# A GLA and Conformer trunk on one core: even tokens first, side taps on one chain, and an earlier rank for a block's last scaling

## The chip, the cores and the metric

The kernel runs on one core of one Trainium2 chip. The metric is the device time of one execution in microseconds (us). A core has five instruction queues that matter here, each working in order: TensorE (PE, matmuls), VectorE (DVE), ScalarE (ACT), GpSimd (POOL) and SyncE (SP), which issues every DMA of this kernel.

## The reference

Two residual layers over 2048 tokens of width 1024, and a last RMSNorm, all in float32:

```python
for i in range(DEPTH):                     # DEPTH = 2
    h = rmsnorm(x, norm_w[i])
    y = gla_mixer(h, ...) if i % 2 == 0 else conv_mixer(h, ...)
    x = x + y
return rmsnorm(x, final_norm_w)

def conv_mixer(h, ...):
    a, gl, z = jnp.split(h @ w_in, 3, axis=-1)
    u = a * jax.nn.sigmoid(gl)
    u = causal_depthwise_conv(u, dw_w) + dw_b          # 31 taps
    u = jax.nn.silu(layernorm(u, ln_w, ln_b))
    return (u * jax.nn.silu(z)) @ w_out
```

The first layer is gated linear attention with four heads in chunks of 64 tokens. The second is the causal convolution module above.

## The kernel before

Activations lie with channels on the partitions and tokens along the free axis. The sequence is done in two halves of 1024 tokens (`hf`), each half in two blocks of 512 (`b`). Every projection is made of three matmuls per pair of 128x128 weights, since both operands are split in a high and a low part (`mm3`, L144): 24 matmuls of 512 columns fill one bank of the pool `ps_mm`, which has three banks. Weights come in units of 256 columns: SP loads `wr` (L123), ACT copies it to `wh` (L124), POOL makes the rest `wl` (L125), one unit ahead of its use.

Up to about 900 us the first layer runs. Its head outputs `g` are transposed on PE (L413), copied by ACT and stored to `g_scratch`, and read back by `out1`, which adds the input again from `xT` and stores `x1_scratch`.

Then the second layer runs, `in2(0)`, `in2(1)`, `out2(0)`, `out2(1)`. In `in2` each channel tile `c` of eight gets a gated `u` (L754, VectorE reads a bank of `ps_mm` and so frees it). The convolution is done for pairs of tokens: `u` holds even tokens in `ue` and odd ones in `uo`, three chains A (16 taps, on `ue`), B (15 taps, on `uo`) and C (16 taps, on `ue+uo` with summed weights) give the even output A+B and the odd output C-A-B. A tap is one multiply-add on VectorE (L638) with its running sum in a bank of the pool `ps_b` (two banks). The first `nside` taps of A and of B are made elsewhere: ACT multiplies (L622, L620) and POOL adds (L624), in SBUF tiles `convA` and `convB`; the chain on VectorE takes that sum up at its first tap (L642). C starts from A's sum in SBUF (L640). POOL adds A+B (L647, `even`); `ue+uo` (L669) is POOL's in the first half and VectorE's in the second. The table `SIDES` gives `nside` by half and tile.

The layer norm over the eight tiles (`centre` L700 to L709, `norm` L727 to L729) runs in the background of later projections. In the second half its norms come while `out2(0)` multiplies; their results `yb` are the operands of `out2(1)`.

`out2(hf)` does two blocks of four units; each project loads `x1` into a tile (L825), adds the bank to it (L838), and sums squares (L842, L844). After the fourth unit `finish` makes the factor of the last RMSNorm on PE and POOL, scales the eight tiles in place (L864) and stores them. Block 0 of either half takes its `x1` tiles from the three `u` buffers and the two `prod` buffers, so block 0 of the second half loads into tiles that block 0 of the first half must first have scaled and stored.

The order of each engine's instructions is made when the kernel is built: the framework plans a timeline from its own durations and takes, among what it holds ready, what ranks highest; `tc.high_priority(offset=n)` puts the instructions inside n places ahead of their place in the program. `pump` hands out the background items by a credit of TensorE time.

Of the kernel before, what the change touches and what calls it, by code (L numbers as in the profile page):

```python
# [13 lines left out]
P = 128  # L14
D = 1024
# [15 lines left out]
SIDES = ((1, 7, 7, 7, 7, 5, 9, 7),  # L31
         (1, 5, 3, 5, 9, 7, 6, 4))
# [8 lines left out]
def kernel(  # L41
    ctx: ExitStack,
    tc: tile.TileContext,
    xT: bass.AP,
    wall: bass.AP,
# [21 lines left out]
    ps_m = ctx.enter_context(tc.tile_pool(name="ps_m", bufs=3, space=bass.MemoryType.PSUM))  # L67

# [296 lines left out]
    def core(hf, h, i, v, sz, qkb, sink):  # L365
# [40 lines left out]
        def turn():  # L406
            g = sink.pop(("g", i))
            if i % 2 == 0:
                sink["t"] = m_bank()
            gt = sink["t"]  # L410
            for c in range(2):
                o = c * 256 + (i % 2) * P
                pe.transpose(gt[:, o:o + P], g[:, c * P:(c + 1) * P], ident)  # L413
            if i % 2 == 1:
                st = t2("st")
                for c in range(2):
                    cs = slice(c * 256, (c + 1) * 256)
                    act.activation(st[:, cs], gt[:, cs], AF.Copy, scale=cc(C_GN, 2 * h + c))
                if h < HEADS - 1:
                    for c in range(2):  # L420
                        r0 = (2 * h + c) * P
                        sp.dma_start(
                            out=gd[hf, r0:r0 + P, (i - 1) * P:(i + 1) * P],
                            in_=st[:, c * 256:(c + 1) * 256])
                else:
                    sink["stage"].append(st)
# [67 lines left out]
    def out1(hf, stage, ahead):  # L494
        a = [[], []]
        for b in range(2):
            if b == 1:
                run_late(0)
            for k in range(KT):
# [6 lines left out]
                else:  # L506
                    for s in range(2):
                        src = stage[b * 2 + s][:, (k - 6) * 256:(k - 5) * 256]
                        ds = slice(s * 256, (s + 1) * 256)
                        act.activation(hi[:, ds], src, AF.Copy)  # L510
                        dve.tensor_tensor(lo[:, ds], src, hi[:, ds].bitcast(F32), ALU.subtract)
                a[b].append((hi, lo))
        accs = [l1p.tile([P, NB], F32, name="acc", bufs=2) for _ in range(2)]
        for pair in range(2):
            ws = [next_unit(12 + 2 * pair), next_unit(13 + 2 * pair)]
            for b in range(2):
                t0 = hf * TH + b * NB
                for ch in range(4 * pair, 4 * pair + 4):
                    xr = l1p.tile([P, 4, 3, CK], F32, name="Q", bufs=2).rearrange("p a b c -> p (a b c)")[:, 0:NB]
                    sp.dma_start(out=xr, in_=xT[ch * P:(ch + 1) * P, t0:t0 + NB])  # L520
# [77 lines left out]
    def conv(hf, c, u, dst, S1):  # L598
# [13 lines left out]
        def side(which):  # L612

            st[which] = l2p.tile([P, NB + 1], F32, name="conv" + which, bufs=2)
            acc = st["p" + which] = st[which][:, 1:NB + 1]
            for m in range(nside):
                src, w = tap(which, m)
                p = acc if m == 0 else l2p.tile([P, NB], F32, name="prod", bufs=2)
                if m == 0 and which == "B":
                    act.activation(p, src, AF.Identity, scale=w, bias=cc(C_DWB, c))  # L620
                else:
                    act.activation(p, src, AF.Copy, scale=w)  # L622
# [3 lines left out]
        def chain(which, m0, m1, n):  # L626
            def fn():
                first = 0 if which == "C" else nside
                if m0 == first:
                    st["ps"] = b_bank()  # L630
                ps = st["ps"]
# [19 lines left out]
        def odd():  # L651
            dve.scalar_tensor_tensor(
                dst[c][:, 1], st["ps"], dwb2[:, c:c + 1], st["B"][:, 1:NB + 1], ALU.add, ALU.subtract)
# [8 lines left out]
        for which, n in (("A", 16), ("B", 15), ("C", 16)):  # L662
            m0 = 0 if which == "C" else nside
# [4 lines left out]
            if which == "A":  # L668
                items.append((0.0, lambda: (pool if hf == 0 else dve).tensor_tensor(ue, ue, uo, ALU.add)))  # L669
            if which == "B":  # L670
                items.append((0.0, even))
        items.append((0.7, odd))
        items.append((0.0, sums))
        side("A")
        side("B")
# [3 lines left out]
    def layernorm(hf, dst, S1, y_out):  # L679
# [41 lines left out]
        def norm(b, k):  # L721
            def fn():
                z = b2()
                sp.dma_start(out=z, in_=szd[hf, k * P:(k + 1) * P, b * NB:(b + 1) * NB])
                zv = z.rearrange("p (t s) -> p s t", s=2)
# [16 lines left out]
    def in2(hf, sched, a, y_out, ahead):  # L742
        dst, S1 = [], []

        def glu(w, u, b):
            with tc.high_priority(offset=PRIO):
# [8 lines left out]
                    u[:, :, o:o + 256].rearrange("p s t -> p t s"),  # L755
                    a_ps.rearrange("p (t s) -> p t s", s=2),
                    sg.rearrange("p (t s) -> p t s", s=2), ALU.mult)
# [46 lines left out]
    def out2(hf, a):  # L804
        for b in range(2):
# [41 lines left out]
            def finish(s):  # L847
                ss = slice(s * n, (s + 1) * n)
                kp = () if ns == 1 else (1, 3, 5) if s else (1, 3, 5, 7)
                with tc.high_priority(offset=1000 if ns > 1 else 0):  # L850
# [6 lines left out]
                for ch, m, t in parts:  # L857
                    for k in range(ch, ch + m):
                        x = xs[k][:, ss]
                        if k in kp:  # L860
                            act.activation(x, x, AF.Copy, scale=cc(C_FW, k))
                            pool.tensor_tensor(x, x, rbs, ALU.mult)
                        else:
                            dve.scalar_tensor_tensor(x, x, cc(C_FW, k), rb, ALU.mult, ALU.mult)  # L864
                    sp.dma_start(
                        out=out[ch * P:(ch + m) * P, t0 + s * n:t0 + (s + 1) * n].rearrange("(c p) t -> p c t", p=P),
                        in_=t[:, :, ss])
# [120 lines left out]
```

## Time and profile before

| | us |
|---|---|
| median of 3 runs | 1676.16 |
| lowest and highest of them | 1675.92, 1680.72 |
| the profiled execution, its own time | 1678.1 |
| its span, first to last instruction | 1676.0 |

All views of the trace come from the profiled execution and count from the start of its span. Names are the program's with buffer numbers left out, L12 is line 12 of the kernel before. "Idle before" names the engine that ended a wait. The granted TensorE clock is given as a share: 1.00 is 2.4 GHz, 0.50 is 1.2 GHz.

### The profile page before, as it was taken

What the parts mean: (1) busy time and instruction counts of PE and PEld (TensorE: products, weight loads), DVE (VectorE), ACT (ScalarE), POOL (GpSimd) and SP (SyncE); (2) the same over time, 40 slices, a digit from 0 to 9 for tenths busy, and PEclk for the clock granted to TensorE, in tenths of its full rate; (3) what the DMA queues carried; (4) which work ended last, traced back from release to release, by engine and by line L of the source; (5) the groups of instructions that cost most, each with busy time, mean ns of one, the idle gap of its engine ahead of it and who ended that gap; (6) DMA issues with size and microseconds to landing.
All of it is one profiled execution on the core that took longest, in us unless ns stands there. A gap on an engine that the chain in (4) does not pass through costs nothing.

```text
span 1676.0 us, 23547 instructions
## 1 busy us (share of the span) xinstructions
PE 1609.4 (96%) x9028; PEld 1410.2 (84%) x9028; DVE 972.7 (58%) x1481; ACT 739.6 (44%) x1246; POOL 900.2 (54%) x787
## 2 busy tenths in 40 slices
PE   8999999999999999999999999999999899999697
PEld 6989999998889999999888887877788678877597
DVE  7433232241434232325243999989699999977634
ACT  6645252342557353415232544443553355435432
POOL 4444343334744333323342989985398798456342
PEclk9999999999999999999999999999999999999798
DMA  6021111144511212123452211225154113643633
GB/s 190 26 83 57 64 51 57 57 139 139 169 45 33 82 51 64 45 63 102 144 164 88 76 38 38 94 70 157 59 174 157 57 45 101 202 163 124 234 115 137
DMA packets 74016, 165.68 MB, mean 99 GB/s; under 512 B 7760, under 2 KB 16464, under 8 KB 73904
## 3 DMA queue, kind: packets, MB, share of 16 engines
q1 hardware_dynamic: 73904, 164.19, 30.5%
q8 instruction: 70, 1.15, 0.3%
q14 instruction: 42, 0.34, 0.1%
HBM read 128.51 MB, written 35.65 MB: 98 GB/s over the span
## 4 chain that ended last, share of the span: by engine, by line
PE 73%; DVE 16%; DMA 3%; ACT 3%; issue 2%; POOL 2%; SPq 0%; POOLq 0%; DVEq 0%; ACTq 0%
PE mm L144 63%; DVE pb L638 10%; PE pb L144 3%; PE pb L388 1%; PE pb L390 1%; DVE pb L642 1%; PE pm L379 1%; DMA wr<-in_wall_dram 1%; PE pm L413 1%; DVE u L754 1%; DVE al L190 1%; PE pm L288 1%; POOL acc L205 1%; DMA u<-x_scratch 1%; DVE pb L640 1%
## 5 line engine op out<-in xcount | busy, mean ns | idle before, releaser
L144 PE MATMUL mm<-ah,wh 128*128 128x512 f32 (+1 forms) x1600 | 595.3, 388 | 44.8 <-DVE u L838 20.4
L144 PE MATMUL mm<-al,wh 128*128 128x512 f32 (+1 forms) x1600 | 592.6, 385 | 0.0
L144 PE MATMUL mm<-ah,wl 128*128 128x512 f32 (+1 forms) x1600 | 590.0, 386 | 0.0
L125 POOL TENSOR_TENSOR wl<-wr,wh 128x1024 fp32r<-128x1024 f32 x140 | 344.0, 2471 | 214.9 <-ACT wh L124 208.9
L144 PEld LDWEIGHTS mm<-ah,wh 128*128 128x128 f32 x1600 | 302.3, 190 | 110.1 <-DVE u L838 20.0
L144 PEld LDWEIGHTS mm<-al,wh 128*128 128x128 f32 x1600 | 302.2, 190 | 57.1 <-issue 0.2
L144 PEld LDWEIGHTS mm<-ah,wl 128*128 128x128 f32 x1600 | 301.4, 190 | 58.0 <-issue 0.2
L144 PE MATMUL mm<-wh,ah 128*128 128x256 f32 x896 | 259.2, 289 | 0.0
L144 PE MATMUL mm<-wh,al 128*128 128x256 f32 x896 | 254.7, 284 | 0.0
L144 PE MATMUL mm<-wl,ah 128*128 128x256 f32 x896 | 254.2, 284 | 0.0
L124 ACT ACTIVATE wh<-wr 128x1024 fp32r<-128x1024 f32 x144 | 145.5, 1051 | 140.9 <-PE mm L144 92.4
L638 DVE SCALAR_TENSOR_TENSOR pb<-u,C,pb 128x512 f32<-128x512 f32 x252 | 184.9, 747 | 0.7
L638 DVE SCALAR_TENSOR_TENSOR pb<-u,dwc,pb 128x512 f32<-128x512 f32 x240 | 179.9, 750 | 1.2
L144 PEld LDWEIGHTS mm<-wl,ah 128*128 128x128 f32 x896 | 171.4, 191 | 0.4
L144 PEld LDWEIGHTS mm<-wh,ah 128*128 128x128 f32 x896 | 171.3, 191 | 0.4
L144 PEld LDWEIGHTS mm<-wh,al 128*128 128x128 f32 x896 | 171.3, 191 | 0.0
L622 ACT ACTIVATE prod<-u,C 128x512 f32<-128x512 f32 x148 | 105.5, 721 | 135.7 <-POOL convA L624 68.4
L624 POOL TENSOR_TENSOR convA<-convA,prod 128x512 f32<-128x512 f32 x74 | 98.3, 1329 | 5.7 <-ACT prod L622 1.6
L624 POOL TENSOR_TENSOR convB<-convB,prod 128x512 f32<-128x512 f32 x74 | 98.0, 1325 | 4.0 <-ACT convB L620 0.7
L397 DVE SCALAR_TENSOR_TENSOR S<-S,dec,pb 128x256 f32<-128x256 f32 x56 | 26.8, 479 | 95.4 <-PE pb L144 95.3
L401 POOL TENSOR_TENSOR ss<-ss,e 128x1 f32<-128x1 f32 x64 | 13.4, 209 | 124.4 <-ACT g L400 124.4
L523 DVE TENSOR_TENSOR Q<-mm,Q 128x512 f32<-128x512 f32 x32 | 22.1, 689 | 93.0 <-PE mm L144 78.3
(195 smaller groups left out, 2174.1 us busy)
## 6 DMA issues: line engine op xcount, KB each, us to landing
wr<-in_wall_dram SPq DMA_DIRECT2D x144, 512.0 KB, 4.1
raw<-in_xT_dram SPq DMA_DIRECT2D x32, 256.0 KB, 3.7
Q<-in_xT_dram SPq DMA_DIRECT2D x32, 256.0 KB, 3.2
x_scratch<-Q SPq DMA_DIRECT2D x32, 256.0 KB, 3.1
sz_scratch<-t SPq DMA_DIRECT2D x32, 256.0 KB, 2.3
b<-sz_scratch SPq DMA_DIRECT2D x32, 256.0 KB, 3.5
g_scratch<-st SPq DMA_DIRECT2D x48, 128.0 KB, 1.9
raw<-g_scratch SPq DMA_DIRECT2D x24, 256.0 KB, 3.5
```

What stands on the lines that cost most here:

```text
L124: act.activation(wh[:, ks, :], raw, AF.Copy)
L125: (dve if i < 2 else pool).tensor_tensor(wl[:, ks, :], raw, wh[:, ks, :].bitcast(F32), ALU.subtract)
L144: pe.matmul(ps, s, m, start=(i == 0), stop=(i == 3 * n - 1))
L190: dve.tensor_tensor(lo, src, hi.bitcast(F32), ALU.subtract)
L205: eng.tensor_tensor(acc, acc, sq, ALU.add)
L288: pe.matmul(ps, wgs[:, k, :], m, start=(n == 0), stop=(n == 15))
L379: pe.matmul(s_ps[:, 0:192], ki[:, js], Q[:, j].rearrange("p s c -> p (s c)"), start=True, stop=True)
L397: dve.scalar_tensor_tensor(S[h], S[h], dec[:, j:j + 1], kv, ALU.mult, ALU.add)
L523: dve.tensor_tensor(xr, ps, xr, ALU.add)
L622: act.activation(p, src, AF.Copy, scale=w)
L624: pool.tensor_tensor(acc, acc, p, ALU.add)
L638: dve.scalar_tensor_tensor(dstm, src, w, ps, ALU.mult, ALU.add)
```

## The change

Three things change. First, tokens are kept even ones first inside each block of 512, from the head outputs on: the transposes of `g` write their columns apart, the stores to `g_scratch` go in rows of 128 elements instead of 256, `out1` reads its residual from a copy `xP` of the input in that order, and the host puts the output back in order. With that `u`, the gate and `z` are read and written in two runs of 256 in place of steps of two. Second, POOL and ACT make side taps for A alone (the table holds about the double of the old one), B starts on VectorE with its bias, A keeps its sum in the bank, VectorE makes the even output from that bank, and C goes on in the same bank; `ue+uo` is POOL's in both halves. Third, the factor of `finish` ranks 1000 ahead in every block, and its scaling and stores rank `PRIO` (80) ahead.

```diff
-SIDES = ((1, 7, 7, 7, 7, 5, 9, 7),
-         (1, 5, 3, 5, 9, 7, 6, 4))
+SIDES = ((2, 14, 14, 14, 14, 10, 15, 14),
+         (2, 10, 6, 10, 15, 14, 12, 8))
...
-                o = c * 256 + (i % 2) * P
-                pe.transpose(gt[:, o:o + P], g[:, c * P:(c + 1) * P], ident)
+                o = (i % 2) * CK
+                gv = gt[:, c * 256:(c + 1) * 256].rearrange("p (s t) -> p s t", s=2)[:, :, o:o + CK]
+                pe.transpose(gv.rearrange("p s t -> p t s"), g[:, c * P:(c + 1) * P], ident)
...
-        def side(which):
+        def side():
...
+            acc = st["pA"] = l2p.tile([P, NB], F32, name="convA", bufs=2)
             for m in range(nside):
-                src, w = tap(which, m)
+                src, w = tap("A", m)
...
                 for m in range(m0, m1):
                     src, w = tap(which, m)
-                    dstm = ps
-                    if m == n - 1 and which != "C":
-                        dstm = st["p" + which]
+                    dstm = st["B"][:, 1:NB + 1] if which == "B" and m == n - 1 else ps
                     if m > first:
                         dve.scalar_tensor_tensor(dstm, src, w, ps, ALU.mult, ALU.add)
-                    elif which == "C":
-                        dve.scalar_tensor_tensor(dstm, src, w, st["pA"], ALU.mult, ALU.subtract)
+                    elif which == "A":
+                        dve.scalar_tensor_tensor(dstm, src, w, st["pA"], ALU.mult, ALU.add)
+                    elif which == "B":
+                        dve.tensor_scalar(dstm, src, w, cc(C_DWB, c), ALU.mult, ALU.add)
                     else:
-                        dve.scalar_tensor_tensor(dstm, src, w, st["p" + which], ALU.mult, ALU.add)
+                        dve.scalar_tensor_tensor(dstm, src, w, ps, ALU.mult, ALU.subtract)
...
-            pool.tensor_tensor(d[:, 0], st["pA"], st["B"][:, 0:NB], ALU.add)
+            dve.tensor_tensor(d[:, 0], st["psA"], st["B"][:, 0:NB], ALU.add)
...
-        for which, n in (("A", 16), ("B", 15), ("C", 16)):
+        for which, n in (("B", 15), ("A", 16), ("C", 16)):
...
-                items.append((0.0, lambda: (pool if hf == 0 else dve).tensor_tensor(ue, ue, uo, ALU.add)))
+                items.append((0.0, lambda: pool.tensor_tensor(ue, ue, uo, ALU.add)))
+                items.append((0.6, even))
...
-                with tc.high_priority(offset=1000 if ns > 1 else 0):
+                with tc.high_priority(offset=1000):
...
-                for ch, m, t in parts:
-                    for k in range(ch, ch + m):
+                with tc.high_priority(offset=PRIO):
+                    for ch, m, t in parts:
+                        for k in range(ch, ch + m):
```

Where the instructions stand now is shown at three places. The first is VectorE in the second half, where one tile's chain ends and the next one's goes on (`d<-pb,dwb` is the odd output, `u<-u` is `ue+uo`, taps with `dwc` are C's). Before:

```order
L638 SCALAR_TENSOR_TENSOR convA<-u,C,pb 128x512
L652 SCALAR_TENSOR_TENSOR d<-pb,dwb_96,convB 128x512
L669 TENSOR_TENSOR u<-u 128x527
L642 SCALAR_TENSOR_TENSOR pb<-u,C,convB 128x512
L640 SCALAR_TENSOR_TENSOR pb<-u,dwc,convA 128x512
L638 SCALAR_TENSOR_TENSOR pb<-u,C,pb 128x512
L638 SCALAR_TENSOR_TENSOR pb<-u,dwc,pb 128x512
```

and now (L637 is a tap, L639 A's first, L641 B's first, L643 C's first, L648 the even output):

```order
L637 SCALAR_TENSOR_TENSOR convB<-u,C,pb 128x512
L637 SCALAR_TENSOR_TENSOR pb<-u,dwc,pb 128x512
L639 SCALAR_TENSOR_TENSOR pb<-u,C,convA 128x512
L653 SCALAR_TENSOR_TENSOR d<-pb,dwb_96,convB 128x512
L648 TENSOR_TENSOR d<-pb,convB 128x512
L641 TENSOR_SCALAR pb<-u,C 128x512
L637 SCALAR_TENSOR_TENSOR pb<-u,C,pb 128x512
L643 SCALAR_TENSOR_TENSOR pb<-u,dwc,pb 128x512
```

Of a tile's three first taps, one has its sum in SBUF (`convA`) now and not three; B starts from `u` and constants alone; the even output has come to VectorE and `ue+uo` has left it.

The second is VectorE in `out2(0)`, with the norms of the second half (`d<-d,pm` are eight scalings of one block by the layer norm's factor, `b<-b,d` products with the gate, `v4n` that factor's first step, `v` that of `finish`, `u<-u,C,pb` and `prod<-prod,C,pb` the last scaling). Before, from the norm factor of block 1 on:

```order
L167 TENSOR_SCALAR v4n<-pm 128x4
L838 TENSOR_TENSOR d<-mm,d 128x512 x3
L167 TENSOR_SCALAR v_14037<-pb 128x4
L727 TENSOR_TENSOR d<-d,pm 128x2x256 x8
L729 TENSOR_TENSOR b_13753<-b_13753,d 128x2x256
L729 TENSOR_TENSOR b_13812<-b_13812,d 128x2x256
...
L844 TENSOR_TENSOR acc<-acc,pb 128x512 x2
L729 TENSOR_TENSOR b_13830<-b_13830,d 128x2x256
...
L729 TENSOR_TENSOR b_13848<-b_13848,d 128x2x256
L864 SCALAR_TENSOR_TENSOR u<-u,C,pb 128x512 x2
...
L864 SCALAR_TENSOR_TENSOR u<-u,C,pb 128x512 x4
L864 SCALAR_TENSOR_TENSOR prod<-prod,C,pb 128x512 x2
```

and now, from the norms of block 0 on to the same factor `v4n`:

```order
L729 TENSOR_TENSOR b_13666<-b_13666,d 128x512
L709 TENSOR_TENSOR S_12023<-S_12023,pb 128x2x256
...
L729 TENSOR_TENSOR b_13721<-b_13721,d 128x512
L844 TENSOR_TENSOR acc<-acc,pb 128x512
L192 TENSOR_TENSOR al<-b_13708,ah 128x512
L865 SCALAR_TENSOR_TENSOR u<-u,C,pb 128x512 x5
...
L865 SCALAR_TENSOR_TENSOR prod<-prod,C,pb 128x512 x2
L844 TENSOR_TENSOR acc<-acc,pb 128x512
L192 TENSOR_TENSOR al<-b_13734,ah 128x512
L838 TENSOR_TENSOR d<-mm,d 128x512
L169 TENSOR_SCALAR v4n<-pm 128x4
```

The eight scalings of block 0 stood behind the norms of block 1, and stand now ahead of that block's factor.

The third is SP's queue at the same place (`wr` are weights, `b<-sz_scratch` gates for the norms, `d` and `u` the loads of `x1`). Before:

```order
L123 DMA wr<-in_wall_dram 128x1024 x3
L825 DMA d<-x_scratch 128x2x512 x4
L123 DMA wr<-in_wall_dram 128x1024
...
L123 DMA wr<-in_wall_dram 128x1024
L865 DMA out_dram<-u 128x2x512
L123 DMA wr<-in_wall_dram 128x1024
L865 DMA out_dram<-u 128x2x512
L825 DMA u<-x_scratch 128x2x512
L865 DMA out_dram<-u 128x2x512
L865 DMA out_dram<-prod 128x512 x2
L825 DMA u<-x_scratch 128x2x512 x2
```

and now:

```order
L724 DMA b_13807<-sz_scratch 128x512
L866 DMA out_dram<-u 128x2x512 x2
L825 DMA u<-x_scratch 128x2x512
L724 DMA b_13816<-sz_scratch 128x512
L866 DMA out_dram<-u 128x2x512
L866 DMA out_dram<-prod 128x512
L825 DMA u<-x_scratch 128x2x512
L866 DMA out_dram<-prod 128x512
L125 DMA wr<-in_wall_dram 128x1024
L724 DMA b_13825<-sz_scratch 128x512
L125 DMA wr<-in_wall_dram 128x1024
L825 DMA u<-x_scratch 128x2x512
```

The stores of block 0's result and the loads into its tiles stand now ahead of two loads of weights and of the loads of `d`.

## Rows read from the trace of the kernel before

**Rows 1.** The page, busy time: us (share of span)
```profile
PE 1609.4 (96%) x9028; PEld 1410.2 (84%) x9028; DVE 972.7 (58%) x1481; ACT 739.6 (44%) x1246; POOL 900.2 (54%) x787
```

**Rows 2.** Stretches: length, busy us by engine, granted TensorE clock, DMA
```profile
0.00:900.00 900.00, 886.88 (x5679) 809.93 (x5680) 328.81 (x583) 398.08 (x755) 371.20 (x420) 1.00 0.29 89
900.00:1000.00 100.00, 100.00 (x453) 83.13 (x451) 76.41 (x105) 41.95 (x59) 70.10 (x55) 1.00 0.13 43
1000.00:1200.00 200.00, 188.68 (x803) 153.24 (x802) 183.69 (x241) 90.73 (x131) 150.51 (x111) 0.97 0.27 85
...
1300.00:1490.00 190.00, 178.46 (x766) 144.95 (x765) 183.66 (x249) 82.44 (x112) 137.20 (x93) 0.98 0.35 111
1490.00:1560.00 70.00, 66.51 (x298) 54.44 (x297) 52.05 (x76) 41.39 (x63) 45.74 (x25) 0.95 0.41 134
1560.00:1590.00 30.00, 13.81 (x56) 11.24 (x55) 18.93 (x28) 9.07 (x15) 8.10 (x4) 0.72 0.79 275
```

**Rows 3.** Waits of TensorE, 900 to 1500: who for whom, us, times, longest
```profile
PE mm L144 <- DVE u L754: 12.6, 6, 4.4
PE mm L144 <- DVE u L838: 4.2, 4, 1.8
PE mm L144 <- ACT t L767: 3.1, 1, 3.1
```

**Rows 4.** Groups by form, 930 to 1676: busy us, mean ns, idle before
```profile
L638 DVE SCALAR_TENSOR_TENSOR pb<-u,C,pb 128x512 f32<-128x512 f32 x248 | 182.3, 747 | 0.7
...
L624 POOL TENSOR_TENSOR convA<-convA,prod 128x512 f32<-128x512 f32 x74 | 98.3, 1329 | 5.7 <-ACT prod L622 1.6 <-ACT convA L622 0.7
...
L640 DVE SCALAR_TENSOR_TENSOR pb<-u,dwc,convA 128x512 f32<-128x512 f32 x16 | 26.0, 1626 | 0.0
...
L754 DVE TENSOR_TENSOR u<-mm,t 128x512 f32<-128x512 f32 x29 | 30.1, 1071 | 2.7 <-PE mm L144 2.7
...
L642 DVE SCALAR_TENSOR_TENSOR pb<-u,C,convB 128x512 f32<-128x512 f32 x15 | 25.7, 1715 | 5.2 <-POOL convB L624 5.2
...
L647 POOL TENSOR_TENSOR d<-convA,convB 128x512 f32<-128x512 f32 x16 | 22.3, 1397 | 27.0 <-DVE convB L638 25.9 <-ACT prod L622 1.2
L642 DVE SCALAR_TENSOR_TENSOR pb<-u,C,convA 128x512 f32<-128x512 f32 x15 | 20.3, 1356 | 0.0
...
L669 DVE TENSOR_TENSOR u<-u 128x527 f32<-128x527 f32 x8 | 11.2, 1399 | 0.0
L669 POOL TENSOR_TENSOR u<-u 128x527 f32<-128x527 f32 x8 | 11.1, 1391 | 0.3 <-DVE convA L638 0.3
...
L838 DVE TENSOR_TENSOR u<-mm,u 128x512 f32<-128x512 f32 x12 | 8.0, 685 | 20.6 <-PE mm L144 14.2 <-DMA u<-x_scratch 6.5
```

**Rows 5.** Waits of VectorE, 1040 to 1200
```profile
DVE pb L642 <- POOL convB L624: 5.2, 1, 5.2
```

**Rows 6.** Chain that ended last, 1540 to 1600: start us, us, what
```profile
1570.08 1.41 DVE u L864 x2
...
1571.50 3.56 DMA out_dram<-u
...
1575.08 6.19 DMA u<-x_scratch
...
1581.36 0.70 DVE u L838
```

**Rows 7.** TensorE alone, 1564 to 1588
```profile
1564.00:1588.00 24.00, 7.81 (x29) 0.64 0.81 280
```

**Rows 8.** Timeline of VectorE, 1480 to 1600: start us, us, what
```profile
1521.21 4.87 DVE L727 TENSOR_TENSOR d<-d,pm 128x512 f32<-128x512 f32 x8 [0.94 <-PE pm L178]
...
1548.70 4.87 DVE L727 TENSOR_TENSOR d<-d,pm 128x512 f32<-128x512 f32 x8 [0.66 <-PE pm L178]
```

**Rows 9.** The stretch 1000 to 1100, all engines
```profile
1000.00:1100.00 100.00, 97.38 (x428) 79.79 (x427) 99.08 (x134) 49.14 (x70) 97.02 (x74) 1.00 0.22 74
```

**Rows 10.** Groups by line, 0 to 930: the transposes of g
```profile
L413 PE MATMUL pm<-ident,g 128*128 128x128 f32 x128 | 24.4, 272 | 0.0
```

More of the change, by code (lines that the diff above doesn't have):

```diff
@@ L44 @@
     xT: bass.AP,
+    xP: bass.AP,
     wall: bass.AP,
@@ L421, in turn @@
                         r0 = (2 * h + c) * P
+                        b, o = i // 4, (i % 4 // 2) * P
                         sp.dma_start(
-                            out=gd[hf, r0:r0 + P, (i - 1) * P:(i + 1) * P],
-                            in_=st[:, c * 256:(c + 1) * 256])
+                            out=gd[hf, r0:r0 + P, b * NB:(b + 1) * NB].rearrange(
+                                "p (s t) -> p s t", s=2)[:, :, o:o + P],
+                            in_=st[:, c * 256:(c + 1) * 256].rearrange("p (s t) -> p s t", s=2))
                 else:
@@ L507, in out1 @@
                     for s in range(2):
[L508 to L511, printed above, removed]
+                        src = stage[b * 2 + s][:, (k - 6) * 256:(k - 5) * 256].rearrange("p (s t) -> p s t", s=2)
+                        h2, l2 = (t.rearrange("p (s t) -> p s t", s=2)[:, :, s * P:(s + 1) * P] for t in (hi, lo))
+                        act.activation(h2, src, AF.Copy)
+                        dve.tensor_tensor(l2, src, h2.bitcast(F32), ALU.subtract)
                 a[b].append((hi, lo))
@@ L519, in out1 @@
                     xr = l1p.tile([P, 4, 3, CK], F32, name="Q", bufs=2).rearrange("p a b c -> p (a b c)")[:, 0:NB]
-                    sp.dma_start(out=xr, in_=xT[ch * P:(ch + 1) * P, t0:t0 + NB])
+                    sp.dma_start(out=xr, in_=xP[ch * P:(ch + 1) * P, t0:t0 + NB])
                     ps = mm_bank()
@@ L610, in tap @@
             return ue[:, m:m + NB], dwc[:, c, m:m + 1]
-        def side(which):
-            st[which] = l2p.tile([P, NB + 1], F32, name="conv" + which, bufs=2)
-            acc = st["p" + which] = st[which][:, 1:NB + 1]
+        def side():
+            acc = st["pA"] = l2p.tile([P, NB], F32, name="convA", bufs=2)
             for m in range(nside):
-                src, w = tap(which, m)
+                src, w = tap("A", m)
                 p = acc if m == 0 else l2p.tile([P, NB], F32, name="prod", bufs=2)
[L619 to L622, printed above, removed]
+                act.activation(p, src, AF.Copy, scale=w)
                 if m > 0:
@@ L652, in odd @@
             dve.scalar_tensor_tensor(
-                dst[c][:, 1], st["ps"], dwb2[:, c:c + 1], st["B"][:, 1:NB + 1], ALU.add, ALU.subtract)
+                dst[c][:, 1], st["psA"], dwb2[:, c:c + 1], st["B"][:, 1:NB + 1], ALU.add, ALU.subtract)
         def sums():
@@ L661, in conv @@
         items = []
-        for which, n in (("A", 16), ("B", 15), ("C", 16)):
-            m0 = 0 if which == "C" else nside
+        for which, n in (("B", 15), ("A", 16), ("C", 16)):
+            m0 = nside if which == "A" else 0
             while m0 < n:
@@ L668, in conv @@
             if which == "A":
-                items.append((0.0, lambda: (pool if hf == 0 else dve).tensor_tensor(ue, ue, uo, ALU.add)))
-            if which == "B":
-                items.append((0.0, even))
+                items.append((0.0, lambda: pool.tensor_tensor(ue, ue, uo, ALU.add)))
+                items.append((0.6, even))
         items.append((0.7, odd))
         items.append((0.0, sums))
-        side("A")
-        side("B")
+        side()
+        st["B"] = l2p.tile([P, NB + 1], F32, name="convB", bufs=2)
         pool.tensor_copy(st["B"][:, 0:1], bcar[:, c:c + 1])
```

39 lines of the change are left out of this document (21 added, 18 removed).

## The prediction

> **What bounds the kernel now.** I read the page first: TensorE is busy 96% of the span [rows 1], so little more than the rest can be won, and the question is where that rest lies. The table of stretches says it [rows 2]. Before 900 us TensorE is idle for 13.1 us of 900. From 1000 to 1200 it lacks 11.3 us and from 1300 to 1490 another 11.5; in both VectorE is busy 183.7 us, 92% and 97% of the stretch. From 1560 to 1590 it lacks 16.2 us, over half of that stretch. These are two different limits, and the change touches both.
>
> The first is the convolution. Of these 22.9 us of TensorE's waits 12.6 and 4.2 end with VectorE [rows 3], which reads a bank of `ps_mm` late because taps stand ahead of that read in its queue; the rest, 6.1, are ACT's, half of it one wait of 3.1. The granted clock falls behind such waits: 0.97 of 200 us and 0.98 of 190 us [rows 2] is another 9.8 us of work at 2.4 GHz not done. So the convolution's stage loses about 32.7 us, and VectorE's share by the waits is 16.8/22.9 of it, 24 us.
>
> The second is one wait. The chain shows it [rows 6]: the last scaling of block 0 on VectorE starts at 1570.1, its first two take 1.41 us, the store from that tile 3.56, the load of new `x1` into it 6.19, the add that frees the bank 0.70; TensorE goes on at 1582.1. From 1564 to 1588 it made 29 matmuls [rows 7], where a stretch without waits makes 453 in 100 us, 0.22 us each [rows 2]; 80 are missing, 17.6 us, of which 16.2 are the wait and the rest the half clock behind it.
>
> **The change, part by part.** VectorE first, per channel tile [rows 4]. The three first taps cost 1.356 (A), 1.715 (B) and 1.626 us (C), each with two operands in SBUF; an ordinary tap, whose sum is in a bank, costs 0.747. Now only A's first tap reads a sum in SBUF. C's starts from the bank: 0.747. B's starts from `u` and two constants, a form that the trace doesn't show; between the add's 0.685 and 1.356 I take 0.747, since its one operand is less than a tap has. That is 4.70 before and 2.85 now, 1.85 less. The even output comes to VectorE; its form is that of the residual add, a bank and an SBUF tile to SBUF, 0.685. The two writes of `u` cost 1.071 each with steps of two; in two runs they are the same add, 0.685 each, 0.77 less, or nothing less if the steps are not what costs. Together 1.93 us less per tile, 31 us for 16 tiles. In the second half eight sums `ue+uo` leave VectorE, 8 x 1.399 = 11.2. The table gives 174 side taps for 180, so VectorE gets six more taps, 4.5 us. In all VectorE loses 37.6 us of work, 13 in the first half and 24 in the second; 25 in all at the worst end of the writes.
>
> That VectorE and POOL take the same for `ue+uo`, 1.399 and 1.391 us, is a row of this trace [rows 4]. The Trainium skill says otherwise (GPSIMD Engine Reference, section Key points): VectorE is about twice as fast at elementwise work. By that rule the eight sums would be an estimated 5.6 us on VectorE and the work taken from it 32 us; the trace differs, with 1.399, and I go by it.
>
> POOL, on the other side: 158 side adds for 148 at 1.329, 16 even outputs at 1.397 less, eight more sums at 1.391 [rows 4]: 4.5 us less in the first half, 6.6 more in the second. In the first half it has no room, busy 97.0 of 100 us from 1000 to 1100 [rows 9]; in the second it has (137.2 of 190, [rows 2]), which covers its 6.6 us. ACT makes six activations fewer and bounds nothing.
>
> What of this reaches the end? In the first half 13 us are freed against a loss of 17.3 (11.3 idle, 6 of clock), in the second 24 against 15.3, and only the part that VectorE ends counts: 12 and 11, 23 us if all goes. I take three quarters, **17 us**: some of TensorE's waits come from single long stays in VectorE's queue that a smaller sum doesn't remove, and A's first tap now needs POOL's whole side sum, where the old chain began after half of it. The stall that VectorE itself had there, 5.2 us for B's side sum [rows 5], goes, as B has none; A's first tap is late next. Bounds: 8 us, if only that stall and the clock behind it go, and 24.
>
> Then the last scaling. By the order rows, the scaling of block 0 stands now ahead of the norm factor of block 1; it stood behind the eight scalings that began at 1548.7 [rows 8]. Counted from the norm of block 0, which ends at 1526.1 [rows 8], sixteen instructions stand before it, at 0.6 (an eighth of 4.87, [rows 8]) to 1.1 us (a write of `u`, [rows 4]) each, 10 to 18 us: it starts at 1536 to 1544. The chain behind it (1.41 + 3.56 + 6.19 + 0.70, 11.9 us) then ends by 1556, before 1565.9 (1582.1 less 16.2), where TensorE ran out of banks. So the wait and its clock go, 17.6 us. I give back 3 us: eight scalings (5.6 us at 0.70) stand ahead of block 0's last splits, and in SP's queue the stores and two loads, which wait for the scaling and for a store of 3.56 us, stand ahead of two loads of weights. Leaves **14.5 us**, between 11 and 17.6. The norms of block 1 come later by some 6 us; they are needed eight projections after TensorE enters `out2(1)`, 8 x 24 x 0.22 = 42 us, and that is their cover. If it is gone, each further us is a wait.
>
> The rest I cost at nothing. The transposes have as many columns as before. The stores of `g` have rows half as long, but they are of heads 0 to 2 and are read only after head 3. `xP` is read as `xT` was. The norms' product with the gate gets plainer steps, below 1 us in all on the path.
>
> The sum: 17 + 14.5 = 31.5 us. Against the profiled execution's span of 1676.0 us that is 1644.5; its own time was 1678.1, but the median of the runs, 1676.16, is what I count from: **1645 us**.
>
> **The rivals.** *POOL takes VectorE's place.* For it: 97.0 of 100 us in the first half [rows 9], and one chain of up to fifteen side taps that must be whole before A starts. Against it: POOL's own sum falls by 4.5 us there, and fifteen taps of B stand before A on VectorE as cover. Then about 3 us of the 17 are left: 1676.2 - 14.5 - 3 = 1659. *The wait at the scaling comes back elsewhere*: the norms of block 1, or the weights behind the stores, are late for `out2(1)`. For it: VectorE, SP and POOL each work in order and all carry both; against: the 42 us of cover. Then only some 2 us of the second part are left: 1676.2 - 17 - 2 = 1657. *The new order doesn't bring what it says*: the builder's plan puts the items in order by its own durations, and where the chip's differ, waits move and don't go. Both parts nearly lost: 1674, no change. *Slower:* the transposes. They now write every column apart by 512 bytes from the one before, a form that no row shows on TensorE. There are 128, at 0.272 us [rows 10], in a stretch where TensorE is busy 886.9 of 900 us [rows 2], so nothing covers them. It decides from 31.5/128 = 0.25 us more for each, nearly a doubling: at twice 0.272 the time is 1676.2 - 31.5 + 34.8 = 1679.5, at three times 1714. Against it: the count of columns and weights is the same, and nothing in the trace ties a matmul's time to where it writes.
>
> **How the numbers follow.** Forecast 0.55, POOL 0.17, wait elsewhere 0.13, no change 0.08, slower 0.07. The forecast's own range is 1635 to 1657 (24 + 17.6 and 8 + 11 us). With the two rivals that keep one part it reaches 1664, and 3 us are added below for a write of `u` or a first tap of B that is cheaper than its bound: 1632 to 1664 holds 0.85. A measurement of this kernel can tell about 0.3%, 5 us, from no change; faster by more than that are the first three cases, 0.85, within it 0.08, slower 0.07.
>
> **What would show it.** In the changed kernel's profile VectorE's busy time is about 935 us (972.7 less 37.6); the writes of `u` take about 0.69 us, C's first tap 0.75, only A's first tap over 1.3. TensorE's waits for the write of `u` fall from 12.6 us to under 5. The wait of 16.2 us is gone, and the scaling of block 0 stands some 10 us behind the norms of that block. Wrong: VectorE waits for `convA` by over 5 us (POOL); TensorE waits as long for the weights or for the splits of `out2(1)` (wait elsewhere); transposes over 0.35 us.

## The result, and the profile after

The changed kernel takes 1653.85 us, the median of 4 runs (1652.13 to 1657.52), against 1676.04 of the kernel before: ratio 0.9866, 95% interval 0.9839 to 0.9892. It is 22.2 us faster, for 31.5 predicted; the time lies in the range. The profiled execution's span is 1650.7 us, for 1676.0, 25.3 less; one execution lies some us off the median.

The page of the changed kernel, its first part (engine, busy us and share of the span, instructions), which answers to [rows 1]:

```profile
PE 1603.1 (97%) x9028; PEld 1406.7 (85%) x9028; DVE 954.5 (58%) x1495; ACT 739.4 (45%) x1244; POOL 889.0 (54%) x789
```

VectorE's busy time falls by 18.2 us, half of the 37.6 that were forecast. The table of stretches (columns as in [rows 2]):

```profile
1000.00:1200.00 200.00, 191.90 (x828) 156.38 (x826) 181.77 (x256) 91.11 (x131) 144.83 (x112) 0.98 0.28 89
1300.00:1490.00 190.00, 186.25 (x805) 152.67 (x804) 176.81 (x257) 81.93 (x115) 132.39 (x90) 0.98 0.36 119
1490.00:1560.00 70.00, 64.15 (x306) 53.06 (x305) 57.44 (x78) 43.68 (x65) 48.34 (x25) 0.98 0.59 202
1560.00:1590.00 30.00, 28.80 (x144) 24.18 (x143) 21.40 (x28) 10.97 (x16) 14.86 (x8) 1.00 0.57 205
```

In both convolution stretches TensorE makes more matmuls than in [rows 2], and in 1560 to 1590 it is busy 28.8 of 30 us, where it was 13.8. The waits of TensorE from 900 us to the end:

```profile
PE mm L146 <- ACT t L767: 4.3, 3, 3.0
PE mm L146 <- DVE u L838: 4.3, 2, 3.1
PE mm L146 <- ACT t L750: 4.1, 3, 1.8
PE pb L168 <- DVE acc L844: 3.9, 2, 2.6
PE mm L146 <- DVE v4n L169: 3.1, 1, 3.1
...
```

In the kernel before, the add into `u` of `out2` headed this list, with the one wait of 16.2 us [rows 6]:

```profile
PE mm L144 <- DVE u L838: 20.4, 5, 16.2
```

That wait is gone, and so are the waits for the write of `u`, 12.6 us in [rows 3]. None that is left is longer than 3.1 us. VectorE's groups by form (busy us, mean ns | idle before):

```profile
L192 DVE TENSOR_TENSOR al<-t,ah 128x512 fp32r<-128x512 f32 x32 | 31.9, 1013 | 4.2 <-ACT ah L191 4.2
L192 DVE TENSOR_TENSOR al<-b,ah 128x512 fp32r<-128x512 f32 x16 | 22.5, 1433 | 0.6 <-ACT ah L191 0.4
L639 DVE SCALAR_TENSOR_TENSOR pb<-u,C,convA 128x512 f32<-128x512 f32 x16 | 19.8, 1238 | 0.5 <-POOL convA L625 0.5
L754 DVE TENSOR_TENSOR u<-mm,t 128x512 f32<-128x512 f32 x29 | 19.3, 684 | 5.4 <-PE mm L146 4.0 <-ACT t L750 1.1 <-ACT prod L623 0.2
...
L201 DVE SCALAR_TENSOR_TENSOR t<-t,C,acc 128x512 f32<-128x512 f32 x16 | 18.1, 1146 | 6.4 <-DMA t<-x_scratch 6.4
...
L641 DVE TENSOR_SCALAR pb<-u,C 128x512 f32<-128x512 f32 x15 | 12.1, 806 | 0.1
L643 DVE SCALAR_TENSOR_TENSOR pb<-u,dwc,pb 128x512 f32<-128x512 f32 x16 | 12.0, 751 | 8.1 <-POOL u L670 8.0
...
L648 DVE TENSOR_TENSOR d<-pb,convB 128x512 f32<-128x512 f32 x16 | 10.9, 679 | 0.0
```

The operations that the change rewrote cost close to what was forecast. VectorE now waits 8.0 us for POOL's `ue+uo` (`u L670`) ahead of C's first tap. What grew are some operations that the change didn't touch, most of all the splits `al` of the norm's output (`al<-b`). In the kernel before, the same view shows them, the splits of the second layer's input (`al<-t`) and its scaling (`t<-t`) so:

```profile
L190 DVE TENSOR_TENSOR al<-t,ah 128x512 fp32r<-128x512 f32 x32 | 28.4, 903 | 0.0
...
L199 DVE SCALAR_TENSOR_TENSOR t<-t,C,acc 128x512 f32<-128x512 f32 x16 | 14.5, 923 | 1.2 <-DMA t<-x_scratch 1.2
...
L190 DVE TENSOR_TENSOR al<-b,ah 128x512 fp32r<-128x512 f32 x16 | 14.1, 927 | 2.8 <-ACT ah L189 2.6
```

One landmark divides the gain: the layer norm's mean of the second half, a group of matmuls on `S` that ends the convolution (the last of 8 starts at the second time of the row). Before, and after the change:

```profile
L693 PE MATMUL pm<-S,ones x8: 590/592/595, 1192.4 to 1491.5; 128*128 128x512 f32 x8
```

```profile
L693 PE MATMUL pm<-S,ones x8: 590/592/697, 1174.6 to 1475.4; 128*128 128x512 f32 x8
```

So 16.1 us are won up to there (17 forecast for the convolution). From there to the end of the span it was 184.5 us (1676.0 - 1491.5) and is 175.3, 9.2 less (14.5 forecast for the last scaling). But the mean doesn't stand at the same amount of work in both: counting the projections' matmuls from a point to the end (number in brackets), 777 lie behind it before,

```profile
1486.70:1676.00 189.30, 147.73 (x792) 0.91 0.44 151
1491.50:1676.00 184.50, 144.06 (x777) 0.91 0.45 153
```

and 792 after the change:

```profile
1475.40:1650.70 175.30, 145.17 (x792) 0.96 0.47 161
```

At equal work, with 792 matmuls left, 11.3 us are won up to that point (1486.7 to 1475.4) and 14.0 behind it (189.3 to 175.3). That looks like the prediction with its first term too large. The experiments say otherwise.

### The profile page after: what moved, and what is told of

Same layout as the page of the kernel before. It is cut to its first block, busy times and chain, and to the rows that moved or that the text cites. A ratio compares the mean times of both kernels' runs of the same rounds, so it can differ in the third digit from the quotient of the medians.

```text
span 1650.7 us, 23585 instructions
## 1 busy us (share of the span) xinstructions
PE 1603.1 (97%) x9028; PEld 1406.7 (85%) x9028; DVE 954.5 (58%) x1495; ACT 739.4 (45%) x1244; POOL 889.0 (54%) x789
## 4 chain that ended last, share of the span: by engine, by line
PE 81%; DVE 6%; ACT 5%; issue 3%; DMA 3%; POOL 1%; SPq 0%; POOLq 0%; DVEq 0%; ACTq 0%
PE mm L146 70%; PE pb L146 3%; DVE al L192 2%; PE pb L390 1%; PE pb L392 1%; DMA wr<-in_wall_dram 1%; ACT d L728 1%; PE pm L381 1%; DVE pb L637 1%; PE pm L416 1%; PE pm L290 1%; ACT wh L126 1%; POOL wl L127 1%; DMA t<-x_scratch 1%; DVE al L273 1%
## 5 line engine op out<-in xcount | busy, mean ns | idle before, releaser
L625 POOL TENSOR_TENSOR convA<-convA,prod 128x512 f32<-128x512 f32 x158 | 207.1, 1312 | 11.7 <-ACT prod L623 5.2
L637 DVE SCALAR_TENSOR_TENSOR pb<-u,C,pb 128x512 f32<-128x512 f32 x274 | 199.5, 747 | 1.0
L637 DVE SCALAR_TENSOR_TENSOR pb<-u,dwc,pb 128x512 f32<-128x512 f32 x240 | 178.1, 748 | 1.3
L623 ACT ACTIVATE prod<-u,C 128x512 f32<-128x512 f32 x158 | 112.6, 721 | 104.8 <-POOL convA L625 104.6
L443 DVE SCALAR_TENSOR_TENSOR vl<-mm,r,vh 128x256 fp32r<-128x256 f32 x48 | 22.8, 483 | 89.3 <-ACT vh L442 89.2
```

What stands on the lines that cost most here:

```text
L443: dve.scalar_tensor_tensor(vl, ps, rr, vh.bitcast(F32), ALU.mult, ALU.subtract)
L625: pool.tensor_tensor(acc, acc, p, ALU.add)
```

## The experiments

"Rest" is the span less the mean's start, as above. "Place" is how many matmuls of projections stand on TensorE, in the builder's order, between that mean and the broadcast that carries the last norm's factor for block 0, on which its scaling waits. In the kernel before, e1_ranks and e3_layout the mean stands 15 matmuls of projections later than in the others; what mean, rest and place are for the point with 792 matmuls left, as in the others, stands there in brackets, and comparisons go by that. "Splits" is the busy time of the 16 splits `al<-b`. Medians are in us; ratios are to the kernel before on the same chip.

| kernel | what it is | median | ratio, 95% interval | mean at | rest | place | splits |
|---|---|---|---|---|---|---|---|
| before | | 1676.0 | | 1491.5 (1486.7) | 184.5 (189.3) | 273 (288) | 14.1 |
| e1_ranks | third part alone | 1679.0 | 1.0005 (0.9993-1.0016) | 1494.3 (1489.5) | 184.7 (189.5) | 222 (237) | 19.3 |
| e2_conv | first and second | 1649.4 | 0.9835 (0.9815-0.9856) | 1474.6 | 173.6 | 218 | 15.0 |
| e3_layout | first alone | 1672.8 | 0.9971 (0.9960-0.9982) | 1488.1 (1483.3) | 182.3 (187.1) | 273 (288) | 14.1 |
| e4_taps | second alone | 1651.0 | 0.9842 (0.9821-0.9863) | 1470.1 | 176.1 | 218 | 17.4 |
| f1_after_again | all three | 1653.0 | 0.9868 (0.9847-0.9888) | 1474.7 | 177.0 | 182 | 22.9 |
| f2_conv_again | as e2 | 1647.0 | 0.9833 (0.9814-0.9853) | 1472.9 | 174.0 | 218 | 15.0 |
| f3_conv_behind | f2, scaling later | 1660.9 | 0.9914 (0.9895-0.9934) | 1471.2 | 184.7 | 288 | 16.5 |
| f4_conv_factor | f2, factor's rank | 1643.3 | 0.9815 (0.9794-0.9836) | 1476.2 | 168.0 | 168 | 14.4 |
| h1_conv_scaling | f2, scaling's rank | 1648.4 | 0.9828 (0.9812-0.9844) | 1473.4 | 170.8 | 218 | 17.1 |
| g1_sum_dve | f4, `ue+uo` on VectorE | 1652.8 | 0.9856 (0.9831-0.9882) | 1477.0 | 175.2 | 206 | 20.9 |
| g2_c_sbuf | f4, A's sum in SBUF | 1663.9 | 0.9916 (0.9890-0.9941) | 1489.3 | 174.4 | 206 | 20.6 |
| g3_taps_factor | f4, old token order | 1643.1 | 0.9800 (0.9775-0.9826) | 1473.5 | 166.4 | 168 | 14.5 |

Mean and rest are of the profiled execution. Its own time lay up to 2.9 us off the median, below it in e4 and f3 and above it in f4, so a difference of 3 us in them says nothing.

### Each part alone

**e1_ranks**, the kernel before with the last hunks of the diff:

```diff
-                with tc.high_priority(offset=1000 if ns > 1 else 0):
+                with tc.high_priority(offset=1000):
...
+                with tc.high_priority(offset=PRIO):
                     for ch, m, t in parts:
```

> The kernel before with the third part alone: the ranks of a block's last scaling and its factors. The prediction's size for it: 14.5 us less, 1661.5 us. The rival from the two traces (up to the layer norm's mean of the second half 16 us are gained, behind it 22.2 - 16.1 = 6 us): the wait of 16.2 us goes, but about 10 us come back in out2, 1670 us, with new waits of TensorE for VectorE's work of the same block's end (the add of a bank, the splits) between 1500 and 1600 us. If ranks and convolution help each other, it is neither: little change here, and e2_conv alone gives less than 16.

Measured: ratio 1.0005, nothing. The wait of 16.2 us did go, and others took its place. TensorE's timeline shows the longest, and under it VectorE's timeline what stood ahead of its end:

```profile
1572.79 1.83 PE L166 MATMUL pb<-ones,acc 128*128 128x1 f32 x8 [10.34 <-DVE acc L844]
```

```profile
1554.88 4.02 DVE L865 SCALAR_TENSOR_TENSOR u<-u,C,pb 128x512 f32<-128x512 f32 x6
1558.83 1.39 DVE L865 SCALAR_TENSOR_TENSOR prod<-prod,C,pb 128x512 f32<-128x512 f32 x2
1560.14 2.29 DVE L844 TENSOR_TENSOR acc<-acc,pb 128x512 f32<-128x512 f32 x3
1562.35 3.07 DVE L727 TENSOR_TENSOR d<-d,pm 128x512 f32<-128x512 f32 x5
1565.34 0.68 DVE L844 TENSOR_TENSOR acc<-acc,pb 128x512 f32<-128x512 f32 x1
1565.93 1.88 DVE L727 TENSOR_TENSOR d<-d,pm 128x512 f32<-128x512 f32 x3
1567.73 4.32 DVE L729 TENSOR_TENSOR b<-b,d 128x512 f32<-128x512 f32 x2
1571.96 0.68 DVE L844 TENSOR_TENSOR acc<-acc,pb 128x512 f32<-128x512 f32 x1
```

TensorE stands in its order at the sum of squares of block 1, for the norm's factor that now has the highest rank. The last add into that sum is the last row, behind the scaling of block 0, the norms of block 1 and two products that take 4.32 us together. The rest of the span is as long as before, 184.7 us for 184.5: what the ranks took away came back whole.

**e2_conv**, the changed kernel with those hunks undone:

> The changed kernel without the third part: even tokens first and side taps of A alone, the old ranks. The prediction's size: 17 us less than before, 1659 us, with the last scaling of block 0 behind the eight norms of block 1 and a wait of some 16 us for it as before. The rival: 1660 by the mean's 16.1 us if the parts add. If the wait at the scaling shrinks or grows by itself when the convolution is earlier, this kernel and e1_ranks together don't add up to the 22 us of both.

Measured: 0.9835, 28.1 us between the medians, more than all three parts together. And the wait of 16.2 us is gone without a rank. On VectorE (timeline of the repeat, f2_conv_again) the scaling of block 0 stands ahead of the norms of block 1:

```profile
1518.76 0.15 DVE L169 TENSOR_SCALAR v<-pb 128x4 f32<-128x4 f32 x1
...
1535.14 4.03 DVE L864 SCALAR_TENSOR_TENSOR u<-u,C,pb 128x512 f32<-128x512 f32 x6
...
1547.71 4.87 DVE L727 TENSOR_TENSOR d<-d,pm 128x512 f32<-128x512 f32 x8 [2.92 <-PE pm L180]
```

In the kernel before it started at 1570.1 [rows 6], behind norms at 1548.7 [rows 8]. Nothing in `out2` was edited. The builder, which plans with its own durations, had put the factor's broadcast 288 matmuls behind the point of equal work; with the shorter convolution it puts it at 218, and the scaling follows. (That the place moved is seen in the order; why the plan came out so is not shown.)

**e3_layout** keeps the old chains and takes the new order of tokens, as in

```diff
-                    u[:, :, o:o + 256].rearrange("p s t -> p t s"),
+                    u[:, :, o:o + 256],
```

> The kernel before with the first part alone: even tokens first, so that the writes of u, the views of the layer norm and the stores of g and the output have other steps. The prediction's terms: 32 writes of u at 0.77 us less each, 25 us of VectorE, of which by 17/37.6 some 11 us reach the end where VectorE bounds: about 1667 us (bounds 1664 to 1676). Rival: the steps are not what costs, the writes stay at 1.07 us: 1676, no change. Slower rival: transposes over 0.35 us instead of 0.27, 1686 or more.

Measured: 0.9971, 4.7 us. (The 0.77 us is for a tile's two writes, so the expectation's 25 us should read 12, and e4's 13 should read 25.) The write of `u` takes 0.680 us for 1.071. The place is that of the kernel before, and the wait for the add is there, 16.3 us.

**e4_taps** keeps the old order of tokens and takes the new chains and table, as in

```diff
-        side("A")
-        side("B")
+        side()
```

> The kernel before with the second part alone: side taps on A alone, first taps of B and C without two operands in SBUF, the even output on VectorE, in the old order of tokens. The prediction's terms: 37.6 - 25 = 13 us less of VectorE (1.16 us less per tile, 11.2 for the sums that go to POOL, 4.5 more for the table), of which some 6 us reach the end: about 1670 us. Rival: it is this part alone that removes the waits, as B's side sum was what VectorE waited for: up to 16 us less, 1660. Slower rival: POOL is the bound now, VectorE waits over 5 us for convA: 1676 or more.

Measured: 0.9842, 26.5 us, nearly all of it, with writes of `u` still at 1.092 us. The first rival holds and falls short, as it had 16 us: the write of `u` is waited for no more, and the place, 218 as in e2, has moved too.

### The ranks on top of the shorter convolution

f1_after_again is the changed kernel, f2_conv_again is e2_conv.

> The changed kernel once more, on the same chip and beside the same runs of before as the next three, to set it against the kernel without the ranks. Theory 1 (the ranks give nothing once the convolution is short): same as f2_conv_again within 2 us, both about 1651. Theory 2 (the ranks cost, as scalings and splits then stand ahead of the adds that free banks): 3 to 5 us above f2_conv_again, 1653 to 1654. Theory 3 (the prediction's: they are worth 11 us or more): 1639 or less against f2's 1650.

> The changed kernel without the third part once more: 1649 to 1651 us by every theory, as e2_conv measured 1649.4; it is the yardstick for f1_after_again, f3_conv_behind and f4_conv_factor.

Measured on one chip: 1652.95 (1651.31 to 1653.73) and 1646.98 (1646.22 to 1648.77, 2 us under what was expected). The third part costs 6 us, as in the first pair (0.9866 against 0.9835). Theory 2. The next two kernels give f2 one rank each, f4 the first line of e1's diff and h1 the second.

> As f2_conv_again, but the factor of the last norm alone has the rank of 1000, the scalings none. Theory 1: same as f2 within 2 us. Theory 2, if it is the scaling's rank that costs in f1: between f2 and f1, nearer to f2; if it is the factor's rank, as TensorE then stands in order at the sum of squares of a block: as f1 or above, with waits of TensorE for acc of over 5 us (10.3 us in e1_ranks).

> As f2_conv_again, but the scaling alone has the rank of 80, its factor none: the fourth corner beside f2 (neither, 1647.0), f4 (factor, 1643.3) and f1 (both, 1653.0). Theory (the scaling's rank costs by itself, 10 us in f1 against f4, as it goes ahead of the adds that free banks): 1653 to 1658, the time from the layer norm's mean to the end 177 us or more for f2's 174. Rival (only both together cost, as the factor must come early for the scaling to be early): 1645 to 1649.

Measured: 1643.28 (1642.88 to 1646.17) for the factor's rank, 3.7 us better than f2, a gain that neither theory had and by which the runs of the two just fail to overlap; 0.9828 for the scaling's rank, the same as f2 (0.9833). My theory of the scaling's rank fell: by itself it costs nothing. Only both together cost. With the factor alone the broadcast is at place 168, the scaling of block 0 starts at 1520.7, and four of the six adds into `d`, which free banks, go ahead of it; in the changed kernel it starts at 1527.6, and three of the six adds into `d` follow it from 1536.7 on, where TensorE waits 3.1 us.

Most of the difference between these two arises there. The same first 242 or 243 matmuls of projections behind the mean, and the rest, take in the changed kernel

```profile
1475.40:1543.60 68.20, 59.12 (x243) 0.97 0.48 158
1543.60:1650.70 107.10, 86.05 (x551) 0.94 0.47 163
```

and in f4

```profile
1476.20:1537.60 61.40, 56.88 (x242) 1.00 0.50 159
1537.60:1644.20 106.60, 85.97 (x551) 0.96 0.48 173
```

6.8 of the 7.3 us lie in the first stretch. TensorE waits there 1.9 and 3.1 us for adds into `d` and 0.8 for weights, in f4 1.2 us in all, and its granted clock is 0.97 for 1.00. One item ahead of the late adds is dear, a split of the norm's output beside POOL's weights (VectorE, and under it POOL):

```profile
1530.92 2.71 DVE L192 TENSOR_TENSOR al<-b,ah 128x512 fp32r<-128x512 f32 x1
```

```profile
1530.69 5.17 POOL L127 TENSOR_TENSOR wl<-wr,wh 128x1024 fp32r<-128x1024 f32 x2 [1.83 <-ACT wh L126]
```

Where POOL stands still a split takes 0.62 us (below), so an estimated 2.1 of the 3.1 us, at most, are this split's. The longest stay of splits comes later and costs TensorE nothing that these stretches show. Timelines of VectorE, and under it of POOL, in the changed kernel:

```profile
1554.97 6.32 DVE L192 TENSOR_TENSOR al<-b,ah 128x512 fp32r<-128x512 f32 x3 [0.40 <-ACT ah L191]
```

```profile
1555.41 5.33 POOL L127 TENSOR_TENSOR wl<-wr,wh 128x1024 fp32r<-128x1024 f32 x2
```

and the same splits in f4_conv_factor, where POOL makes no weights between 1554.7 and 1563.6:

```profile
1557.06 2.48 DVE L192 TENSOR_TENSOR al<-b,ah 128x512 fp32r<-128x512 f32 x4
```

Three splits take 6.32 us beside POOL's weights, four take 2.48 without; yet no wait of TensorE in the changed kernel's list ends with a split. Over the 16 splits the changed kernel pays 22.5 to 22.9 us and f4 14.4. Among the six kernels with the factor's rank and the new chains the rest rises with the splits: 166.4 and 168.0 us at 14.5 and 14.4, 174.4 and 175.2 at 20.6 and 20.9, 175.3 and 177.0 at 22.5 and 22.9. That is a correlation and shows no cause: the place differs too (168, then 182 and 206), in g1 and g2 most of the price lies elsewhere (below), and a kernel that moves POOL's weights alone away from the splits was not tried.

### The place of the scaling

**f3_conv_behind** hands block 0's finish to the builder two units later:

```diff
-                    if u == 3:
+                    if u == 3 and hf == b == 0:
+                        later.append(finish)
+                    elif u == 3:
                         finish(s)
+                if u == 1 and later and (hf, b) == (0, 1):
+                    later.pop()(0)
```

> As f2_conv_again, but the last scaling of block 0 of out2(0) and its factor are handed to the builder two units later, so that on VectorE they stand behind the eight norms of block 1 as in the kernel before. Theory A (with the short convolution the place of the scaling is what took the wait of 16.2 us away, and is worth the 9 to 11 us that e2_conv gains behind the mean): the wait for the add into u is there again, 8 to 16 us, and the time is 1657 to 1661. Theory B (VectorE has 16 us less behind it, so the place doesn't matter): wait under 5 us, 1649 to 1652.

Measured: 1660.93, 14 us more than f2, and the rest is 184.7 us for 174.0. The place is that of the kernel before, 288. Theory A by its time, though the wait is another. TensorE's timeline:

```profile
1555.67 1.84 PE L168 MATMUL pb<-ones,acc 128*128 128x1 f32 x8 [12.19 <-DVE acc L846]
```

With the old place most of the old price is back, convolution short or not. At equal work the convolution's parts win 13 to 16 us behind the mean (e2, e4, f2, against 189.3); of f2's 15.3 some 10.7 are the place's, and where the other 4.6 come from stays open.

### What VectorE's time is worth

The last three go out from f4_conv_factor, on another chip; the kernel before takes 1675.69 us there and 1675.35 on f4's. **g1_sum_dve**:

```diff
-                items.append((0.0, lambda: pool.tensor_tensor(ue, ue, uo, ALU.add)))
+                items.append((0.0, lambda: (pool if hf == 0 else dve).tensor_tensor(ue, ue, uo, ALU.add)))
```

> As f4_conv_factor, but the eight sums ue+uo of the second half are on VectorE again, as in the kernel before. Theory (VectorE's time in the convolution sets the end, at about half its value as in the prediction, 17 of 37.6 us): 11.2 us more on VectorE, about 5 us up to the layer norm's mean of the second half, 1648 us. Rival (VectorE waits 8.0 us for just these sums on POOL before C's first tap, so moving them back costs nothing): 1643, and the wait for the write of ue+uo is gone.

Measured: 1652.76, 9.5 us more. But the mean is at 1477.0, 0.8 later than in f4: in the convolution the 11.1 us cost nothing. The rival is right so far, and in part for its reason: VectorE waits 3.0 us for sums on POOL ahead of C's first tap, for 8.0 in f4. But the sums moved the builder's plan (place 206 for 168), and the price, which neither theory had, is paid behind the mean, most of it at one place. VectorE's timeline, and under it TensorE's:

```profile
1595.03 4.04 DVE L864 SCALAR_TENSOR_TENSOR u<-u,C,pb 128x512 f32<-128x512 f32 x6 [4.54 <-PE pb L180]
```

```profile
1600.86 0.36 PE L146 MATMUL mm<-ah,wh 128*128 128x256 f32 x1 [3.73 <-DVE d L838]
```

The adds into `d` stand behind eight scalings, and the clock is 0.72 from 1600 to 1605. f4 runs from 1595 to 1605 without a wait.

The sums took 1.391 us each on VectorE in the mean, as on POOL in [rows 4]. But the mean is of unlike ones (least, median and most, ns):

```profile
L670 DVE TENSOR_TENSOR u<-u x8: 690/1319/2408, 1241.7 to 1457.5; 128x527 f32<-128x527 f32 x8
```

The last of them, at 1457.5, finds POOL idle and takes 0.69 us, half of POOL's 1.38 for its eight sums in the first half. So the rule that VectorE is about twice as fast at such work (the Trainium skill, GPSIMD Engine Reference, section Key points) does show there, and not in the mean beside a busy POOL.

**g2_c_sbuf** gives C's first tap and the even output two operands in SBUF again:

```diff
+                    if which == "A" and m == n - 1:
+                        dstm = st["pA"]
...
-                        dve.scalar_tensor_tensor(dstm, src, w, ps, ALU.mult, ALU.subtract)
+                        dve.scalar_tensor_tensor(dstm, src, w, st["pA"], ALU.mult, ALU.subtract)
...
-            dve.tensor_tensor(d[:, 0], st["psA"], st["B"][:, 0:NB], ALU.add)
+            dve.tensor_tensor(d[:, 0], st["pA"], st["B"][:, 0:NB], ALU.add)
```

> As f4_conv_factor, but A's last tap writes to SBUF, and C's first tap and the even output read it from there, as in the kernel before: two operands in SBUF again. Theory (the operand's place is the price): C's first tap 1.5 to 1.7 us for 0.75, the even output 1.2 to 1.4 for 0.68, in all 20 to 25 us more of VectorE, at half its value 10 us, 1653 us, with waits of TensorE for the write of u. Rival (the place of the operand doesn't count for itself; what counted was that a chain has one side sum): both under 0.9 us, 1643.

Measured: 1663.90, 20.6 us more, where the theory had 10. Its groups by form:

```profile
L645 DVE SCALAR_TENSOR_TENSOR pb<-u,dwc,convA 128x512 f32<-128x512 f32 x16 | 25.4, 1585 | 11.2 <-POOL u L672 11.2
L650 DVE TENSOR_TENSOR d<-convA,convB 128x512 f32<-128x512 f32 x16 | 22.3, 1393 | 0.0
```

The operand's place is the price: 0.83 us more for the tap, 0.71 for the even output, 24.7 us in all. The mean is at 1489.3, 13.1 later than in f4, and later than the kernel before at equal work (1486.7); TensorE waits for the write of `u` again (3.8 us), and behind the mean the plan and the wait of 3.7 us are those of g1. C's first tap had this form before the change; the even output had not, as POOL made it. So the run shows that such operands can cost the whole gain of the convolution, and not that nothing else made it.

**g3_taps_factor** is f4 without the new order of tokens.

> As f4_conv_factor, but with the tokens in the old order: second part and the factor's rank alone. Theory from e2_conv and e4_taps (0.9835 and 0.9842): the order of tokens takes 12 us from VectorE but adds 0 to 2 us of gain once no write of u is waited for, so 1643 to 1646. Rival (it is worth what it is alone, 0.3%): 1648.

Measured: 1643.07, 0.9800 for f4's 0.9815: the same. The order of tokens takes 11 us off the writes of `u` (30.7 to 19.4 in the second layer from 930 us on) and adds nothing once no write of `u` is waited for. f4 and g3, about 2% below the kernel before, are the fastest here.

## Why the prediction was right, and where it was wrong

The time lay in the range and the sign was right; of the two terms one was right in its place and too large, and one was credited to the wrong part.

- **The first limit, VectorE in the convolution: right; its term of 17 us: too large, within its bounds of 8 and 24.** At equal work the changed kernel gains 11.3 us up to the mean, e2 and f2 12 to 14.
- **Its operations: right.** First taps 1.238, 0.806 and 0.751, 2.80 us per tile for 2.85; even output 0.679 for 0.685; writes of `u` 0.684 for 0.685; VectorE waits 0.5 us for `convA`, the sign that the POOL rival named. It does wait for POOL elsewhere, 8.0 us for `ue+uo`, where it waited 5.2 for B's side sum; with the second half's sums back on VectorE (g1) the mean comes no earlier. Transposes 0.272 us as in [rows 10], so the slower rival had no ground.
- **VectorE's sum, 37.6 us: missed.** 18.2 came. The step that failed is that all else keeps its price: splits of the norm's output went from 14.1 to 22.5 us, splits of the second layer's input from 28.4 to 31.9, and its scaling from 14.5 to 18.1, 15.5 us in all. That VectorE and POOL take the same for `ue+uo` was read from a mean, too: of the eight behind 1.399 us one took 0.71, the longest 2.4.
- **That a freed microsecond counts at about one rate, as three expectations took it from the prediction's sums (17 of 37.6): wrong.** In the convolution 24.7 us back on VectorE cost 13 (g2), 11.1 cost 0.8 (g1), and the 11 of the writes of `u` nothing (g3). Only in g2 does TensorE wait for the write of `u` again.
- **The last scaling, 14.5 us: wrong in its cause.** "So the wait and its clock go, 17.6 us. I give back 3": alone the ranks give back all of it (e1). The wait went because the shorter convolution moved the factor's broadcast in the builder's order (e2, e4), and with that done the ranks cost 6 us (f1 against f2). The prediction took the order rows of the changed kernel for the work of the ranks; the order of a kernel with the first two parts alone would have shown the scaling ahead of the norms of block 1 already. The scaling did stand about where it was forecast, at 1527.6, 14 us behind block 0's norms.
- **The rival "the wait at the scaling comes back elsewhere" (0.13) is what e1 did**, at the sum of squares and not at the norms or the weights that it named. Its 42 us of cover did hold: no wait for the splits of block 1 is in the changed kernel's list of waits.
- **The range** held in part by luck. Behind the mean 14.0 us came at equal work for 14.5, but from the convolution's parts, which alone give 15.3 there (f2); the ranks, to which they were put down, added nothing. The median's gain of 22.2 us is 9.3 short of the sum.

## What to carry to other kernels

Where a builder sets the order by its own durations, an edit in one stage moves instructions in another. Before crediting a part with what the order rows show, look at the order with that part left out, and undo each part on the chip. A higher rank for a result helps as far as what feeds it is ready: the factor's rank alone gained 3.7 us behind the short convolution, and both ranks gained nothing behind the old one, where TensorE then stood waiting for the sum (e1). And count, for every VectorE instruction, how many of its operands are in SBUF before counting elements. A landmark for dividing a gain has to stand at the same amount of work in both kernels.

## What the runs showed of the hardware

The size of one effect was not expected. A VectorE split of 128x512 with both operands in SBUF takes 0.62 us where POOL stands still (four in 2.48, f4) and 2.1 on average beside POOL's weight splits (three in 6.32, the changed kernel); POOL's own two take 5.33 there. Taps with the sum in a bank of PSUM stay at 0.747 to 0.752 us in the kernel before, the changed one, e2 and e4, whatever POOL does.

The Trainium skill says so (SBUF — State Buffer, section Who interferes with whom): a VectorE instruction with two SBUF inputs contends with a GpSimd instruction that reads SBUF, and one with at most one SBUF input, outside the 2-port performance modes, does not. The rows above agree. The prediction had the first taps' 1.4 to 1.7 us from rows and needed no rule for them. It didn't ask where the unchanged splits would fall beside POOL, and by this rule it should have.
